# RMSNorm with swish on one core: wider rows for one load and one store, fewer and later stores, and two row sums on ScalarE in every third unit

**Chip, cores, metric.** One core of one Trainium2 chip. The metric is the device time of a run in microseconds, lower is better. "Span" is the profiled time from the first to the last instruction; it lies about 1.3 us under the time of the same run.

## The reference

```python
batch, seq, dim = 16, 1024, 512          # x: fp32, 16384 rows of 512
rms = np.sqrt(np.mean(x ** 2, axis=-1, keepdims=True) + eps)
x_norm = x / rms * gamma
return x_norm * (1.0 / (1.0 + np.exp(-x_norm)))
```

Every row is read once and written once: 33.56 MB in, 33.56 MB out.

## The kernel before

The 16384 rows lie 128 to a "row" of all partitions, so a core-wide row is 2 KB a partition and 256 KB in all; there are 128 of them. They pass through a ring of 96. SyncE issues the loads, ScalarE the stores. The work goes by units of four rows (`cn = 4`, 32 units).

```python
sizes = [4, 4, 8] + [16] * 6 + [8, 8]     # rows of each load, and of the store that answers to it
ring, cn, n_sq = 96, 4, 3
...
def square(k):                            # ScalarE
    t, at, first = chunks[k]
    if first:
        nc.scalar.wait_ge(ld[t], 16)      # the whole load must have landed
    acc = nc.scalar.activation(           # row 3: square and sum in one instruction
        out=junk[k % 2], in_=xb[:, at + n_sq, :], func=AF.Square,
        scale=inv_d**0.5, accum_out=ms[:, k, n_sq : n_sq + 1])
    ...
    square = nc.scalar.activation(        # rows 0 to 2: squares to PSUM
        out=sq[k % 2][:, 0:n_sq, :], in_=xb[:, at : at + n_sq, :],
        func=AF.Square, scale=inv_d**0.5)
...
for k in range(K + 3):                    # ScalarE's order
    if k < K:
        square(k)
    while stored < T and ends[stored] <= k - 2:
        store(stored)                     # waits until its units' Silus are done
        stored += 1
    if 2 <= k < K + 2:
        swish(k - 2)                      # Silu of four rows
...
# VectorE: sums(k), a reduce of the three squared rows, then norm(k - 1), four row multiplies.
# GpSimd: eps and the power -1/2. A load into ring rows in use waits for their stores.
```

## Time and profile before

| | before |
|---|---|
| time | 160.11 us (159.87 to 160.23, 3 runs) |
| span | 158.7 us |
| VectorE, ScalarE busy | 87%, 79% of the span |
| both DMA queues | 99.2% of 16 engines' span, 423 GB/s |

The costliest groups of the page, which the change touches. The columns are line, engine, operation, names and shapes, count, busy us and mean ns, then idle time ahead of them and what ended it.

```profile
L184 ACT ACTIVATE xb<-xb 128x2048 f32<-128x2048 f32 x32 | 61.1, 1909 | 17.8 <-DVE xb L224 17.8
L213 DVE TENSOR_REDUCE ms<-sq 128x3 f32<-128x1536 f32 x32 | 56.1, 1754 | 7.0 <-ACT sq L172 7.0
L165 ACT ACTIVATE junk<-xb 128x512 bf16<-128x512 f32 x32 | 19.7, 615 | 3.4 <-DMA xb<-in_x_dram 3.3
```

VectorE's reduce waits once, at the start. ScalarE has 17.8 us of waits for VectorE ahead of its Silus: some room for more sums. The waits for loads are 3.3 us, all at the start.

### The profile page before, as it was taken

Reading aid. Unit: us, or ns where it says so; the run is one execution under the profiler, and the core shown is the slowest. Engines: PE = TensorE matmul, PEld = TensorE weight load, DVE = VectorE, ACT = ScalarE, POOL = GpSimd, SP = SyncE. Lnnn points to the kernel's source line nnn. Section 1 sums busy time; section 2 is a strip of 40 time slices with the busy share of each in tenths; the row PEclk is TensorE's granted clock in tenths of the full one; section 3 lists DMA queues with packets and bytes.
Section 4 is the critical chain, followed back from the end, with each engine's and each line's share of the span. In section 5 each row is a group of like instructions: output and inputs, shape, how many; then the busy total and the mean of one; then the engine's idle time right before and its main releaser. Section 6 shows DMA issues by size and latency. Waiting matters only on the chain.

```text
span 158.7 us, 439 instructions
## 1 busy us (share of the span) xinstructions
DVE 138.9 (87%) x162; ACT 125.3 (79%) x129; POOL 65.4 (41%) x71
## 2 busy tenths in 40 slices
DVE  0249999999999999999999999999999999999300
ACT  0935989888888889988888888888998888883600
POOL 2035444444455555544444445555544444445000
DMA  7999999999999999999999999999999999999997
GB/s 235 427 523 405 396 450 419 409 452 407 460 394 413 467 421 452 413 396 479 432 413 429 446 429 413 425 417 458 429 454 396 434 446 438 446 413 438 388 458 301
DMA packets 3324, 67.15 MB, mean 423 GB/s; under 512 B 501, under 2 KB 501, under 8 KB 505
## 3 DMA queue, kind: packets, MB, share of 16 engines
q1 hardware_dynamic: 1584, 33.56, 49.9%
q10 hardware_dynamic: 1736, 33.57, 49.3%
q14 instruction: 4, 0.02, 0.0%
HBM read 33.56 MB, written 33.56 MB: 423 GB/s over the span
## 4 chain that ended last, share of the span: by engine, by line
DVE 85%; DMA 5%; ACT 1%; issue 1%; POOL 0%; POOLq 0%
DVE xb L224 53%; DVE ms L213 32%; DMA gamma<-in_gamma_dram 5%; ACT xb L184 1%; DVE gamma_sb L237 0%; POOL gamma L142 0%; POOL blank L141 0%; POOLq L65 0%
## 5 line engine op out<-in xcount | busy, mean ns | idle before, releaser
L224 DVE SCALAR_TENSOR_TENSOR xb<-xb,rstd,gamma_sb 128x512 f32<-128x512 f32 x128 | 87.4, 748 | 0.0
L184 ACT ACTIVATE xb<-xb 128x2048 f32<-128x2048 f32 x32 | 61.1, 1909 | 17.8 <-DVE xb L224 17.8
L213 DVE TENSOR_REDUCE ms<-sq 128x3 f32<-128x1536 f32 x32 | 56.1, 1754 | 7.0 <-ACT sq L172 7.0
L147 POOL TENSOR_SCALAR aeps<-ms 128x4 f32<-128x4 f32 x32 | 20.6, 644 | 75.2 <-DVE ms L213 75.2
L172 ACT ACTIVATE sq<-xb 128x1536 f32<-128x1536 f32 x32 | 45.9, 1433 | 0.0
L154 POOL TENSOR_TENSOR rstd<-aeps,neg_half 128x4 f32<-128x4 f32 x32 | 44.0, 1376 | 2.7
L165 ACT ACTIVATE junk<-xb 128x512 bf16<-128x512 f32 x32 | 19.7, 615 | 3.4 <-DMA xb<-in_x_dram 3.3
L165 ACT ACTIVATION_READ_ACCUMULATOR junk<-xb 128x1 f32 x32 | 6.0, 186 | 0.0
L199 ACT ACT_TABLE_LOAD x1 | 1.3, 1283 | 3.6 <-issue 3.6
L237 DVE LOAD_MASK_SELECT gamma_sb<-gamma x1 | 0.0, 14 | 2.3 <-DMA gamma<-in_gamma_dram 2.3
L141 POOL MEMSET blank<- 128x16 f32 x1 | 0.1, 111 | 1.5 <-POOLq L65 1.5
L237 DVE STREAM_SHUFFLE gamma_sb<-gamma 128x512 f32<-128x512 f32 x1 | 0.7, 717 | 0.0
L142 POOL MEMSET gamma<- 128x512 f32 x1 | 0.5, 524 | 0.0
L264 POOL MEMSET const-float32-0.0<- 128x1 f32 x1 | 0.1, 98 | 0.2 <-issue 0.2
L264 POOL MEMSET const-bfloat16-1.0<- 128x1 bf16 x1 | 0.1, 102 | 0.0
L264 POOL MEMSET const-uint8-127<- 128x1 uint8 x1 | 0.1, 101 | 0.0
L143 POOL MEMSET neg_half<- 128x4 f32 x1 | 0.1, 101 | 0.0
L264 POOL MEMSET const-float32-1.0<- 128x1 f32 x1 | 0.1, 98 | 0.0
## 6 DMA issues: line engine op xcount, KB each, us to landing
xb<-in_x_dram SPq DMA_DIRECT2D x6, 4096.0 KB, 41.9
out_dram<-xb ACTq DMA_DIRECT2D x6, 4096.0 KB, 31.1
xb<-in_x_dram SPq DMA_DIRECT2D x3, 2048.0 KB, 35.0
out_dram<-xb ACTq DMA_DIRECT2D x3, 2048.0 KB, 10.7
xb<-in_x_dram SPq DMA_DIRECT2D x2, 1024.0 KB, 5.8
out_dram<-xb ACTq DMA_DIRECT2D x2, 1024.0 KB, 20.8
scratch<-blank ACTq DMA_DIRECT2D x1, 8.0 KB, 7.7
gamma<-in_gamma_dram ACTq DMA_DIRECT2D x1, 8.0 KB
```

Source lines behind the costliest of these rows:

```text
L141: nc.gpsimd.memset(blank, 0.0).then_inc(s_blank, 1)
L142: nc.gpsimd.memset(gamma4, 0.0).then_inc(s_zero, 1)
L147: nc.gpsimd.tensor_scalar(out=aeps[:, k, :], in0=ms[:, k, :], scalar1=eps_f, scalar2=None, op0=ALU.add,),
L154: nc.gpsimd.tensor_tensor(out=rstd[:, k, :], in0=aeps[:, k, :], in1=neg_half, op=ALU.pow),
L165: acc = nc.scalar.activation(out=junk[k % 2], in_=xb[:, at + n_sq, :], func=AF.Square, scale=inv_d**0.5, accum_out=ms[:, k, n_sq : n_sq + 1],)
L172: square = nc.scalar.activation(out=sq[k % 2][:, 0:n_sq, :], in_=xb[:, at : at + n_sq, :], func=AF.Square, scale=inv_d**0.5,)
L184: nc.scalar.activation(out=rows, in_=rows, func=AF.Silu), s_norm, k + 1
L199: nc.scalar.preload_act_table_set("silu_and_others")
L213: nc.vector.tensor_reduce(out=ms[:, k, 0:n_sq], in_=sq[k % 2][:, 0:n_sq, :], op=ALU.add, axis=mybir.AxisListType.X,),
L224: ins = nc.vector.scalar_tensor_tensor(out=row, in0=row, scalar=rstd[:, k, j : j + 1], in1=gamma_sb, op0=ALU.mult, op1=ALU.mult,)
L237: nc.vector.stream_shuffle(gamma_sb, gamma4, [0] * 32), s_gld, 16
L264: nc = _bacc.Bacc("TRN2", target_bir_lowering=False, num_devices=1)
```

## The change

Its intent: relieve VectorE, which has no gap, by one row in every third unit, and move the same bytes in fewer and larger packets (11 loads and 11 stores become 9 and 8). Loads and stores no longer pair; groups of up to 48 rows lie together in HBM. Below, a "64 KB row" is what one partition moves in a transfer of 32 of the kernel's rows (32 x 2 KB).

```diff
-    sizes = [4, 4, 8] + [16] * 6 + [8, 8]
+    groups = [16, 48, 32, 16, 16]
+    loads = [(0, 0, 4), (0, 4, 4), (0, 8, 8), (1, 0, 16), (1, 16, 16), (1, 32, 16),   # group, row, rows
+        (2, 0, 32), (3, 0, 16), (4, 0, 16)]
+    stores = [(0, 0, 16), (1, 0, 32), (1, 32, 16), (2, 0, 16), (2, 16, 16), (3, 0, 16),
+        (4, 0, 8), (4, 8, 8)]
-    n_sq = 3
+    def n_sq(k):
+        return 2 if k % 3 == 2 else 3
 ...
+        rows = ap[begin[g] * P : (begin[g] + groups[g]) * P]
+        return rows.rearrange("(p n) d -> p n d", n=groups[g])[:, r : r + n, :]
 ...
-        acc = nc.scalar.activation(out=junk[k % 2], in_=xb[:, at + n_sq, :], ...)
+        for j in range(n, cn):
+            acc = nc.scalar.activation(out=junk[j % 2], in_=xb[:, at + j, :], ...)
```

(Cut to its core: the semaphores, the waits for ring rows and the store's arguments follow the lists.)

## The prediction

> **What bounds the kernel now.** I read the page from the top: engines, then the 40 slices, then the chain that ended last, then the DMA queues. The first and the third seem to say VectorE.
>
> ```profile
> span 158.7 us, 439 instructions
> DVE 138.9 (87%) x162; ACT 125.3 (79%) x129; POOL 65.4 (41%) x71
> ...
> DMA  7999999999999999999999999999999999999997
> ...
> DMA packets 3324, 67.15 MB, mean 423 GB/s; under 512 B 501, under 2 KB 501, under 8 KB 505
> ...
> q1 hardware_dynamic: 1584, 33.56, 49.9%
> q10 hardware_dynamic: 1736, 33.57, 49.3%
> ...
> DVE 85%; DMA 5%; ACT 1%; issue 1%; POOL 0%; POOLq 0%
> ```
>
> VectorE has no gap between 11.0 us and 148.15 us: the chain repeats four row multiplies (2.65 us) and one reduce (1.67 us), 4.32 us for a unit of four rows, 32 times. But the two DMA queues add up to 99.2% of 16 engines' span, and the DMA row is full in every slice but the first and last. Two resources are saturated together. Which of them sets the end is read where VectorE stops: the stretches of the trace, with columns for the stretch, its length, busy VectorE, ScalarE and GpSimd, granted clock, DMA share and GB/s, and the last instructions in order of time.
>
> ```profile
> 60.00:130.00 70.00, 70.00 (x82) 62.74 (x65) 32.73 (x33) 1.00 1.01 433
> 130.00:157.00 27.00, 18.14 (x23) 15.58 (x15) 8.16 (x8) 1.00 0.99 427
> ```
> ```profile
> 143.15 0.34 ACTq L189 DMA_DIRECT2D out_dram<-xb  x1
> ...
> 148.17 1.91 ACT L184 ACTIVATE xb<-xb 128x2048 f32<-128x2048 f32 x1 [0.74 <-DVE xb L224]
> 150.11 0.34 ACTq L189 DMA_DIRECT2D out_dram<-xb  x1
> ```
>
> VectorE and ScalarE are done at 150.1, yet the DMA stays full at 427 GB/s to 157. By the semaphores' landings in the trace the last four stores end at 139.3, 149.0, 153.8 and 158.7 us: 9.7 us for the second (16 rows a partition, 4 MB) and 4.85 us for each of the last two (8 rows, 2 MB). The last store was issued at 150.1, three microseconds before the one ahead of it had landed. So stores are queued at the end, and the DMA engines, not VectorE, set the time. The record of single packets agrees: summed over both queues, the packets of one engine take 157.4 us, and the time from the first packet (1.0 us) to the end of the last (158.3) is 157.3 us.
>
> **What a packet costs.** In the same record one packet is one partition's row of a transfer: 8 KB take 309 ns, 16 KB 611 ns, 32 KB 1213 ns (medians; loads and stores alike). The differences give 302 ns per 8 KB, that is 27.2 GB/s for an engine, and some 8 ns for the packet itself. 64 KB should take about 2418 ns (my extrapolation).
>
> **What the Trainium skill says.** (1) "DMA: Bandwidth & Descriptors", section "Where 436 GB/s comes from": 16 ports of 32 B at 850 MHz give 435.2 GB/s. The trace agrees: 433 GB/s from 60 to 130 us, and 27.2 GB/s an engine. Nothing is left to win on the rate. (2) The same page, "Queues, rings and completion order": each engine takes turns between queue rows, one packet at a time. The trace agrees: while 32 KB loads meet 8 KB stores (24 to 44 us) the shares are near four to one, in the next lines (queue, packets, MB, share); with 32 KB on both sides they are near equal (64 to 78 us: 49.3% and 52.2%).
>
> ```profile
> q1 hardware_dynamic: 224, 6.82, 78.9%
> q10 hardware_dynamic: 226, 1.72, 20.3%
> ```
>
> (3) "VectorE: DVE Perf Modes", "Rules for kernel authors": a reduce runs at 1x; with that page's 0.96 GHz, 512 elements are 533 ns. The trace fits: 1754 ns for 1536 elements is 1600 plus 154. (4) "ScalarE: Activation LUTs", "What ACT_TABLE_LOAD costs": 0.833 ns per element, so a row is 427 ns. The trace fits: 1433 ns for 1536 and 1909 for 2048 differ by 476 for 512, the two writing to different memories.
>
> **The change, part by part.**
>
> Row sums: units 2, 5, ... 29, ten in all, reduce two rows instead of three. VectorE loses 10 x 0.533 = 5.3 us. ScalarE gains ten accumulating squares (615 + 186 ns, of which about 0.19 overlaps, so 0.61 us by their distance from the next square) and loses ten rows of the plain square (0.43 us): +0.19 us a unit, +1.9 us of elapsed work, about +3.7 us in its busy sum. Would ScalarE hold VectorE up? Now ScalarE waits 0.46 us a unit before its Silu, and works 3.86 of 4.32 us. Where VectorE's interval shrinks to 3.79 us and ScalarE still owes the next unit 3.86 us plus handover, I expect a stall of about 0.2 us, once in three units: 0 to 2 us. VectorE then ends at 148.15 - 5.3 + (0 to 2) = 142.8 to 144.8 us, if no load is late.
>
> Transfers: per engine, eight packets for each transfer. Before: 32 of 8 KB, 48 of 16 KB, 96 of 32 KB: 32 x 309 + 48 x 611 + 96 x 1213 = 155.66 us. After: loads 16 of 8 KB, 8 of 16 KB, 40 of 32 KB, 8 of 64 KB; stores 16 of 16 KB, 40 of 32 KB, 8 of 64 KB: 16 x 309 + 24 x 611 + 80 x 1213 + 16 x 2418 = 155.33 us. Saving 0.33 us. Five transfers fewer drop five semaphore writes of 9 ns on each engine, 0.05 us. All of this lies on the saturated path. The bytes are the same.
>
> Does the queue stay full? My own reckoning, with 0.605 us per row of all partitions (1213 ns x 8 / 16). The first store now goes out after four units, near 30.5 us instead of 18.0; loads fill the time. It shares with loads until about 52 us and frees the first ring rows. The 32-row load then runs alone; the 32-row store is issued near 63.5 us and takes equal turns with it in 64 KB packets. That load lands near 75 us and unit 16 wants it at 78.3 (its time now) - 5 x 0.53 = 75.6: tight. Meanwhile the store's other rows meet the 16-row load at two to one, to about 95 us; then the last load is released, lands near 120 us, and is wanted at 125. From there four stores and a remainder queue up. The last store is issued at 145 to 147 us, or 149 with a stall at unit 16, while its turn comes only near 153. At no point do I find an empty queue.
>
> Sum: 160.11 - 0.33 - 0.05 = 159.7 us. The 5.3 us of VectorE are hidden behind transfers and become a longer wait of the last store.
>
> **The rivals.**
>
> VectorE is the bound: the chain gives it 85% of the span, and it has no gap. Then 5.3 us less gives 154.8, or 156.8 with the stalls. Against it: 67.1 MB at 435.2 GB/s alone are 154.2 us, plus 1.0 before the first packet, plus the packets' 8 ns and the slow first ones (8 KB loads average 354 ns rather than 309), plus 1.4 us between span and time. The chain is followed to an instruction and does not show the queue behind the last store.
>
> The 32-row load comes late: unit 16 stalls, ScalarE is held in its queue, two Silus and a store behind it wait. For: my reckoning leaves 0.5 us. Against a loss: at that time the 32-row store keeps the DMA busy for some 20 us, and the end has 4 to 8 us of slack. Even 3 us of stall leaves 159.7; only some 8 us would show, giving 161 to 163.
>
> 64 KB packets are worse than extrapolated (split, or slower in HBM because group pieces now lie 96 KB apart). At 3% on the 32 rows each way, 64 of 256 rows, that is 1.2 us: 160.9. Nothing in the profile speaks for it, as 8 to 32 KB are linear; nothing shows 64 KB either.
>
> Smaller transition costs: packets over the median cost about 0.7 us after the first 5 us, most of it between 20 and 50 us where stores first meet loads. Later, larger stores may save or add 0.3 us of that.
>
> **Range and chances.** Point 159.7. Transitions and spread of runs (159.87 to 160.23) give 0.4 either way, the packet rival stretches the top: 159.0 to 160.6. Over 2% faster needs 156.9, under what the bytes and the start allow in practice: 2%. Over 2% slower needs 163.3, thus an idle DMA of 3 us: 3%. Within: 95%.
>
> **What would show it.** Right: DMA full in every middle slice, both queues near 98.5 to 99.5% together, 2604 packets (3324 less 720), 64 KB packets near 2418 ns, VectorE's busy time near 133.6 us and ScalarE's near 129, the last Silu ending near 145 to 147 and the last store taking 11 to 14 us to land instead of 8.6. Wrong: a DMA slice below 9 in the middle, a last store that lands within 7 us of its issue (then compute sets the end), or 64 KB packets above 2450 ns.

## The result

The changed kernel takes 162.63 us (162.19 to 162.86, 4 runs) against 160.17 (159.87 to 160.28): a ratio of 1.0153, 95% interval 1.0127 to 1.018. Executions over 1.5% slower than the fastest of the same kernel are left out of the means. Ratios here are the mean time of one kernel's fast runs over that of the other's of the same rounds, so not quite the ratio of the medians quoted. The change costs 1.5%; the prediction had 159.7 and at most 160.6.

The page of the changed kernel:

```profile
span 161.5 us, 451 instructions
DVE 134.5 (83%) x162; ACT 126.4 (78%) x149; POOL 65.4 (41%) x71
...
DMA  7999999989999979969999999999999999999994
...
DMA packets 2603, 67.15 MB, mean 416 GB/s; under 512 B 420, under 2 KB 420, under 8 KB 424
...
q1 hardware_dynamic: 1296, 33.56, 49.8%
q10 hardware_dynamic: 1304, 33.57, 48.5%
...
DVE 55%; ACT 25%; DMA 5%; issue 4%; another core or an unknown queue 3%; POOL 0%; ACTq 0%; POOLq 0%
```

The two queues have 720 packets fewer, as intended, and VectorE is busy 4.4 us less. The DMA row has an 8, a 7 and a 6 in the middle, which by the letter is one of the prediction's signs of being wrong. But the row books a packet's whole time in the slice where it begins, and a 64 KB packet takes 2.4 us of a slice of 4.0. Counted by overlap from the record of packets, no slice between the first and the last is under 0.98. So the DMA has work up to the last slice and still sets the end, but the rate fell from 423 to 416 GB/s, and its last slice is at 4 where it was at 7. The share of q10 and q1 is now 98.3%. The stretches of the trace where this arises, before:

```profile
66.00:106.00 40.00, 40.00 (x48) 35.92 (x38) 19.56 (x19) 1.00 0.99 428
156.00:158.00 2.00, 0.00 (x0) 0.00 (x0) 0.00 (x0) 1.00 0.79 336
158.00:160.00 2.00, 0.00 (x0) 0.00 (x0) 0.00 (x0) 1.00 0.00 0
```

and after (the share of engines is next to last, GB/s last; a packet is counted where it begins):

```profile
66.00:106.00 40.00, 34.72 (x42) 32.23 (x38) 16.42 (x17) 1.00 0.97 401
106.00:130.00 24.00, 23.70 (x30) 22.48 (x28) 12.26 (x12) 1.00 1.00 433
158.00:160.00 2.00, 0.00 (x0) 0.00 (x0) 0.00 (x0) 1.00 0.67 287
160.00:162.00 2.00, 0.00 (x0) 0.00 (x0) 0.00 (x0) 1.00 0.02 8
```

Two things are to be seen. From 66 to 106 us, while the 64 KB store takes turns with loads, the DMA counts as busy and moves 401 GB/s instead of 428. From 106 us on it is at 433 again. And at the end the engines stop one after another: 0.67 of them busy, then 0.02.

The record of single packets says the same. A packet's excess is its time over the median of its size. Summed and divided by 16 it grew from 1.42 to 3.17 us an engine, of which 1.6 us lie between 85 and 106 us. From 66 to 106 us alone the excess was 0.1 us before and is 1.9 now, and most of that is not on the 64 KB packets: 1.13 us fall on the 32 KB loads (1339 ns in the mean there), 0.46 on the 64 KB stores, 0.32 on the last 64 KB loads. The last store's 16 landings (one from each engine) came from 157.90 to 158.66 us before and from 158.98 to 161.41 after: the first engine finishes 1.1 us later, the last 2.75 us later. I rebuilt which engine ran which packet by joining each packet to the one whose end it follows (the trace does not name the engine, so this is exact only where ends differ). By that, the mean engine ends at 159.60 us instead of 157.94 (+1.66) and the last at 161.08 instead of 158.29 (+2.79, which is the 2.75 us of the span).

VectorE gained nothing, because the 32-row load came late. The waits of the changed kernel (engine and line, waited for, total us, times, longest) and the order of time around unit 16:

```profile
DVE ms L229 <- ACT sq L187: 12.2, 4, 7.0
ACT junk L178 <- DMA xb<-in_x_dram: 8.8, 4, 5.3
```
```profile
77.58 0.63 ACT L178 ACTIVATE junk<-xb 128x512 bf16<-128x512 f32 x1 [5.35 <-DMA xb<-in_x_dram]
...
79.67 1.76 DVE L229 TENSOR_REDUCE ms<-sq 128x3 f32<-128x1536 f32 x1 [4.84 <-ACT sq L187]
```
```profile
150.00 1.91 ACT L199 ACTIVATE xb<-xb 128x2048 f32<-128x2048 f32 x1 [0.74 <-DVE xb L240]
151.94 0.34 ACTq L204 DMA_DIRECT2D out_dram<-xb  x1
```

The load's 16 landings came from 73.3 to 77.5 us, and the unit needs all of them. ScalarE waits 5.35 us for it, VectorE 4.84 us for ScalarE, and the last store is issued at 151.9 us, later than before (150.1). This still is not what set the end here: the store ahead of it landed from 154.1 to 156.6 us, so every engine had work.

### The profile page after: what moved, and what is told of

The parts are those of the page before. It is cut to its first block, busy times and chain, and to the rows that moved or that the text cites. A ratio compares the mean times of both kernels' runs of the same rounds, so it can differ in the third digit from the quotient of the medians.

```text
span 161.5 us, 451 instructions
## 1 busy us (share of the span) xinstructions
DVE 134.5 (83%) x162; ACT 126.4 (78%) x149; POOL 65.4 (41%) x71
## 2 busy tenths in 40 slices
DMA packets 2603, 67.15 MB, mean 416 GB/s; under 512 B 420, under 2 KB 420, under 8 KB 424
## 4 chain that ended last, share of the span: by engine, by line
DVE 55%; ACT 25%; DMA 5%; issue 4%; another core or an unknown queue 3%; POOL 0%; ACTq 0%; POOLq 0%
DVE xb L240 35%; DVE ms L229 20%; ACT xb L199 12%; ACT sq L187 9%; DMA gamma<-in_gamma_dram 5%; ACT junk L178 4%; DVE gamma_sb L253 0%; POOL gamma L151 0%; POOL blank L150 0%; ACTq L175 0%; POOLq L69 0%
## 5 line engine op out<-in xcount | busy, mean ns | idle before, releaser
L229 DVE TENSOR_REDUCE ms<-sq 128x3 f32<-128x1536 f32 (+1 forms) x32 | 50.8, 1586 | 13.3 <-ACT sq L187 12.2
L187 ACT ACTIVATE sq<-xb 128x1536 f32<-128x1536 f32 (+1 forms) x32 | 41.6, 1299 | 0.0
L178 ACT ACTIVATE junk<-xb 128x512 bf16<-128x512 f32 x42 | 25.8, 615 | 8.8 <-DMA xb<-in_x_dram 8.8
L178 ACT ACTIVATION_READ_ACCUMULATOR junk<-xb 128x1 f32 x42 | 7.8, 186 | 0.0
## 6 DMA issues: line engine op xcount, KB each, us to landing
out_dram<-xb ACTq DMA_DIRECT2D x2, 2048.0 KB, 10.5
```

The source lines that it names most:

```text
L178: acc = nc.scalar.activation(out=junk[j % 2], in_=xb[:, at + j, :], func=AF.Square, scale=inv_d**0.5, accum_out=ms[:, k, j : j + 1],)
L187: square = nc.scalar.activation(out=sq[k % 2][:, 0:n, :], in_=xb[:, at : at + n, :], func=AF.Square, scale=inv_d**0.5,)
L229: nc.vector.tensor_reduce(out=ms[:, k, 0 : n_sq(k)], in_=sq[k % 2][:, 0 : n_sq(k), :], op=ALU.add, axis=mybir.AxisListType.X,),
```

## The experiments

All kernels are the changed one with its lists edited, so that the kernel before is one case of it; all gave correct results. Diffs are against the changed kernel unless said. My theory (A), from the two traces, was that 64 KB packets stretch at the turns between the queues and put the engines out of step. Rivals were the later first store (B) and ScalarE's sums (C). An engine is out of step when it is in a load while most others are in a store, or the reverse. Runs 1 to 4, 5 to 8, 9 to 12 and 13 to 17 each shared a chip, with the kernel before timed beside them. Of its 50 timed runs in all, 48 took 159.80 to 160.69 us; two, on the chip of runs 9 to 12, took 161.73 and 167.56, so a stray long run needs no wide row.

**1. No 64 KB row.**

```diff
-    loads  = [... (2, 0, 32), ...]
-    stores = [(0, 0, 16), (1, 0, 32), ...]
+    loads  = [... (2, 0, 16), (2, 16, 16), ...]
+    stores = [(0, 0, 16), (1, 0, 16), (1, 16, 16), ...]
```

> The changed kernel with its 32-row load and its 32-row store each cut into two of 16 rows (32 KB packets), all else kept. Theory A (64 KB packets stretch at the turns between queues and spread the engines apart): back to 160.0 to 160.8 us, packets' excess over their medians near 1.5 to 2.2 us an engine instead of 3.2, last store's 16 landings within 1.2 us instead of 2.4. Rival B (the later first store, which is kept here, costs it): stays at 162 to 162.9 us. Rival C (two sums on ScalarE, kept here): stays at 162 to 162.9 us.

160.53 us (160.29 to 160.77), ratio 1.0020 (1.0003 to 1.0037). Excess 1.64 us an engine, landings 158.02 to 158.99. The loss is nearly all gone, with the sums and the late first store kept: B and C fall as main causes.

**2. Three sums on VectorE, 64 KB rows kept.**

```diff
-        return 2 if k % 3 == 2 else 3
+        return 3
```

> The changed kernel with three sums on VectorE in every unit, as before. Theory A and B: 162.2 to 163.2 us, since the DMA sets the end; VectorE ends later, and if unit 16's wait is kept, the last store may be issued near 156 and begin to show, up to 164. Rival C (ScalarE's extra sums cost it): 160.0 to 160.5 us.

160.22, 162.57, 160.43, 161.53, 161.27 and 162.45 us; ratio 1.0076 (1.0032 to 1.012). Neither theory foresaw such a spread. The profiled execution was the fastest. The interval lies above 1, so the wide rows cost time without the sums too, and just below the changed kernel's (1.0127 to 1.018), so the sums may have a part in the loss; how is not shown. Runs 10 and 11 look at this kernel again.

**3. The two sums alone, transfers as before.**

```diff
-    groups = [16, 48, 32, 16, 16]
+    groups = [4, 4, 8, 16, 16, 16, 16, 16, 16, 8, 8]
+    loads = stores = [(i, 0, groups[i]) for i in range(11)]
```

> The kernel before with only the two sums in every third unit; transfers as before. Theory A and B: 159.7 to 160.4 us, VectorE ends 3 to 5 us earlier and the last store waits that much longer. Rival C: 162 us or more. If VectorE were the bound: 155 to 157 us.

160.37 us, ratio 1.0006 (0.9985 to 1.0026). ScalarE's last Silu, which waits for VectorE's last row, and the last store:

```profile
145.67 1.91 ACT L197 ACTIVATE xb<-xb 128x2048 f32<-128x2048 f32 x1 [0.74 <-DVE xb L238]
147.61 0.34 ACTq L202 DMA_DIRECT2D out_dram<-xb  x1
```

Against 148.17 and 150.11 before: the last store is issued 2.5 us earlier (I had expected 3 to 5 for VectorE) and the time stays. Compute is not the bound, and relieving it gains nothing.

**4. One first store of 16 rows (and rows in groups of 16), nothing else of the change.**

```diff
+    groups = [16] * 8, loads of 4, 4, 8, then 16 each, 8, 8; stores of 16, ..., 16, 8, 8; n_sq = 3
```

> The kernel before with one first store of 16 rows in place of 4, 4 and 8 (groups of 16 rows), three sums in every unit, no 64 KB row. Theory A: 160.0 to 160.7 us. Rival B (loads alone until 30 us, then a 32 KB store meets them: the 0.7 us stretch at 33 us in the changed kernel): 161 to 162.6 us.

160.70 us, ratio 1.0032 (1.001 to 1.0053): 0.3%, and the cost of the first store meeting the loads is seen (0.9 us of excess from 25 to 60 us, against 0.5 from 10 to 60 before). Not all of the 0.3% is that: the last 8-row load came at 136.8 us and the last store ran late. B is a small part.

**5. Same pieces and packets, other distance in HBM.**

```diff
-    groups = [16, 48, 32, 16, 16]
+    groups = [16, 32, 16, 32, 16, 16]      # the 64 KB rows of the store now lie one behind the other
```

> The changed kernel with the same pieces, order and packet sizes, but the group of 48 rows cut into groups of 32 and 16, so that the 64 KB store rows lie one behind the other in HBM (64 KB from partition to partition, not 96 KB). Theory P (the 96 KB pitch makes store packets collide in HBM): falls to 160.0 to 160.8 us and the excess of the 64 KB store packets between 85 and 105 us goes. Theory A (64 KB turns as such): stays at 161.8 to 163 us.

161.93 us (161.24 to 163.27), ratio 1.0121 (1.0088 to 1.0154). Lower than the changed kernel on that chip (run 8), intervals apart, but two thirds of the loss stay. The distance is not the main cause.

**6. Only the 64 KB store.** The load is cut in two as in run 1.

> The changed kernel with only the 32-row load cut in two; the 64 KB store stays. Unit 16 should no longer wait (its 16 rows land near 62 us, the time wanted is 72). If the 64 KB store, or its meeting with 32 KB loads, makes the loss: 161.5 to 163 us. If the late 64 KB load makes it: 160.2 to 160.8 us, like the run without 64 KB rows.

162.09 us (161.5 to 162.77), ratio 1.0124 (1.0101 to 1.0147). The store alone makes most of the loss. In the profiled execution 14 engines ended by 158.3 us, two at 159.6 and 159.8.

**7. Only the 64 KB load.** The store is cut in two as in run 1.

> The changed kernel with only the 32-row store cut in two; the 64 KB load stays, now meeting 32 KB stores from 47 us on, so it takes two thirds of the turns and lands near 68 to 72 us. If the 64 KB load makes the loss: 161.5 to 163 us. If the 64 KB store does: 160.2 to 160.8 us. If both are needed: both this and the run with the store alone stay under 161 us.

161.18 us (161.0 to 162.06), ratio 1.0084 (1.0064 to 1.0105). A loss, but another one. The load, two thirds of the turns or not, landed at 78.9 us, unit 16 waited 6.7 us, and the last store was issued at 153.4. Stretches of this kernel:

```profile
153.00:156.00 3.00, 0.00 (x0) 0.34 (x1) 0.00 (x0) 1.00 0.74 311
156.00:158.00 2.00, 0.00 (x0) 0.00 (x0) 0.00 (x0) 1.00 1.14 483
158.00:160.00 2.00, 0.00 (x0) 0.00 (x0) 0.00 (x0) 1.00 0.41 172
```

The DMA share falls to 0.74 of 3 us; by overlap the mean engine is idle for 0.6 us from 153 to 155, and for another 0.6 near 138, ahead of an earlier store. The last store lands 6.3 us after its issue, all engines within 0.15 us (159.49 to 159.64), and the packets' excess is only 1.58 us. Here compute sets the end, by way of the late load.

**8. The changed kernel again.**

> The changed kernel itself once more, on the same chip as these runs, for a second trace. All theories: 162.2 to 162.9 us, excess of packets near 3 us an engine, unit 16 waiting some 5 us for the 32-row load. If the slow turns are a matter of chance in the engines' phase (as three sums with 64 KB rows, 160.2 to 162.6, suggest), some of its six runs will lie under 161.5.

162.85 to 163.14 us (4 runs), ratio 1.0180 (1.0167 to 1.0194). Excess 2.62 us, landings 158.16 to 161.49. No run under 161.5, so this kernel loses each time, while run 2's loses at times. By the rebuilt order the mean engine ends here at 158.91 us (+0.97 over the kernel before) and the last at 161.17: the same loss as in the first trace, with a larger part of it in the spread.

**9. A second 64 KB store.**

```diff
     loads as in run 1
-    stores = [..., (2, 0, 16), (2, 16, 16), ...]
+    stores = [..., (2, 0, 32), ...]
```

> No 64 KB load, but a second 64 KB store (the two stores of 16 rows after it joined into one of 32 rows, issued near 113 us while the last load runs until about 125). If 64 KB store rows meeting 32 KB loads stretch packets on some engines: at or above the run with one such store (162.1), 162.0 to 163.5 us, with new excess after 113 us. If that run's loss was only the phase in which its one store began: no more than 162.1, and no excess after 113 us.

161.82 us (161.16 to 162.07), ratio 1.0093 (1.0073 to 1.0113). No more than with one such store, and no excess from 106 to 130 us. My dose argument failed: the second store, of whose 128 packets 44 began before the last load packet, costs nothing that can be seen.

**10 and 11. Two more looks at run 2's kernel.**

> The changed kernel with three sums in every unit, a second time, to look at one execution; its six earlier ones spread from 160.2 to 162.6 us and the one profiled was the fastest. If the slowest engine's stretched packets set the time: an execution of 162 us or more shows a last store whose 16 landings spread over 2 us or more and an engine with 3.5 us of excess or more; one under 160.7 shows a spread near 1 us and at most 2.2 us.

> The same kernel a third time, same expectation: time less 159.1 us should be near the excess of the slowest engine less 1.5 us, within 0.6 us.

162.70 and 163.62 us, two long executions to set beside run 2's of 160.22. The program is the same but the chip is not: the first lies by the top of run 2's fast runs (162.57), the second over it. In the first, VectorE never waited for a late load and the last store was issued at 149.9 us. Its end:

```profile
156.00:158.00 2.00, 0.00 (x0) 0.00 (x0) 0.00 (x0) 1.00 0.73 311
158.00:160.00 2.00, 0.00 (x0) 0.00 (x0) 0.00 (x0) 1.00 0.17 74
160.00:162.00 2.00, 0.00 (x0) 0.00 (x0) 0.00 (x0) 1.00 0.04 16
```

A sixth of the engines are at work from 158 to 160 us. Thirteen engines ended at 158.2 us or earlier, down to 157.3, three between 160.1 and 161.0. The mean engine ended at 158.1 us (158.0 in the short one), with 1.8 us of excess (1.7); so the slowest, by its end, had some 4.7 us (2.3). The landings spread over 3.7 us (0.94). This is the plainest view of the loss: one program, the same mean, 2.5 us more for three late engines. In the second, one engine ended at 161.9 and the other 15 at 159.6 to 159.7. There the last store was issued at 153.8, after a late load; by the rebuilt order the 15 were idle for 0.9 to 2.3 us before it and the late one not at all. So both losses of runs 6 and 7 are in it, but the late engine alone set the time.

**12. A try at something better than both.**

```diff
+    groups = [16] * 8; loads and stores of 4, 4, 8, then 16 each, 8, 8; two sums in every third unit
```

> A try at a version better than both: rows in groups of 16, loads of 4, 4 and 8 rows from one group (the changed kernel's start, whose first packets had 0.5 us of excess against 0.7), early stores of 4, 4 and 8 rows as before (which met the loads with 0.5 us in all against 0.7 to 1.1), no 64 KB row, two sums in every third unit. 159.8 to 160.2 us, so at best 0.2% under the kernel before and likely not clear of it.

160.16 us, ratio 0.9999 (0.9987 to 1.0011). Equal to the kernel before. No version beat it.

Open after twelve runs was whether the 64 KB store does harm by its size or by the empty store queue ahead of it (about 56 to 64 us), after which stores begin anew beside loads (theory G).

**13. The gap without 64 KB rows.**

```diff
     loads and stores as in run 1
+    ends[1] = ends[2]        # rows 16 to 31 are stored only when rows 32 to 47 are done too
```

> No 64 KB row at all, but the store of rows 16 to 31 held back until the unit at which the changed kernel's 64 KB store goes out (near 64 us), so the store queue is empty from about 56 to 64 us as it is in the changed kernel. Theory G (stores that begin anew beside a stream of loads put the engines out of step): 161.3 to 162.5 us, landings of the last store over 2 us apart. Theory A' (the gap alone is harmless, 64 KB packets are needed): 160.3 to 160.8 us, landings within 1.3 us.

160.39 us (160.25 to 160.66), ratio 1.0020 (1.0008 to 1.0032); landings 157.85 to 159.30, 1.45 us apart where I had expected 1.3 at most. The gap is nearly harmless.

**14. The 64 KB store without the gap.**

```diff
     loads as in run 1, stores as in the changed kernel
+    ends[0] = 8              # the first store is held back and still runs when the 64 KB store is issued
```

> The run with the 64 KB store and no 64 KB load, but the first store held back to unit 8 (near 47 us), so that it still runs when the 64 KB store is issued at 64 us and the store queue has no gap. Theory G: 160.2 to 160.9 us. Theory A': 161.5 to 162.8 us, as with the gap.

163.62 us (163.27 to 164.13), ratio 1.0222 (1.0204 to 1.0241); excess 3.15 us, landings 159.16 to 161.91. Worse than with the gap, which I had not expected. Theory G falls; of the two it is the wide rows. Why holding back the first store costs more is not shown.

**15. Run 6 again, as control.**

> Control on this chip: the kernel with the 64 KB store, no 64 KB load, gap kept. 161.5 to 162.8 us as before under either theory.

Fast runs 160.64 to 162.31 us, ratio 1.0090 (1.0053 to 1.0127), and one of 163.75 counted as slow. It is as scattered as run 2; I had not expected runs as low as 160.64. Runs 13 and 15 are the closest pair of all: the same chip, the same loads, and 8 MB of stores that go out at the same unit, as two transfers of 32 KB rows or as one of 64 KB rows. So neither the gap nor the amount that is queued makes the loss. The width of a row and the size of a transfer still change together; no run separates them.

**16. Store packets of 48 KB.**

```diff
     loads as in run 1
-    stores = [(0, 0, 16), (1, 0, 32), (1, 32, 16), ...]
+    stores = [(0, 0, 16), (1, 0, 24), (1, 24, 24), ...]
```

> No 64 KB row; the group of 48 rows is stored as 24 and 24 (48 KB packets) while the loads stay at 16 rows or fewer. If the loss grows with the size of the store packet: between, 160.8 to 162 us. If it needs 64 KB: 160.2 to 160.8 us.

Fast runs 163.65 to 165.52 us, ratio 1.0290 (1.0252 to 1.0327), two more runs at 166.99 and 168.37. Neither branch came true: two stores of 48 KB rows cost more than one of 64 KB rows. They meet loads one after the other here, from 56 to 115 us. The profile fell on the slowest run and shows another end than the runs above: the last store is issued at 160.8 us and lands everywhere within 0.15 us, after loads that landed only at 115.1 and 136.9 us, and the DMA stood nearly idle from about 138 to 146. The store of rows 64 to 79 had landed on its first engine at 127.7 us and on its last at 137.1. The fast runs have no trace, so the reason of their loss stays open, and this run says nothing sure about the width of rows.

**17. Only a late 64 KB store.**

```diff
     loads as in run 1
-    stores = [(0, 0, 16), (1, 0, 32), (1, 32, 16), (2, 0, 16), (2, 16, 16), ...]
+    stores = [(0, 0, 16), (1, 0, 16), (1, 16, 16), (1, 32, 16), (2, 0, 32), ...]
```

> Stores of 16 rows as in the run without 64 KB rows, but those of the group of 32 joined into one 64 KB store, issued near 113 us beside the last load only (to about 127 us), then alone. If every 64 KB store that takes turns with 32 KB loads loses in proportion to its turns: a third of its packets do, 160.6 to 161.2 us. If only the early, longer one does: 160.2 to 160.6 us. If the 64 KB store alone is enough: 161.5 us or more.

160.30 us, ratio 1.0014 (0.9999 to 1.0028). It costs nothing measurable. But the trace shows that this run did not test what I meant: the store's first packet began at 118.8 us and the last load packet at 118.7, so no wide row took turns with a load. In the changed kernel all 128 packets of the 64 KB store, from 67.7 to 95.9 us, began while loads were running. A wide store that meets no load is harmless; how much meeting it takes to do harm, run 9's second store (44 of 128 packets, no loss seen) bounds only from one side.

The runs by their last store's landings (us of the profiled execution, so beside that execution's time):

| kernel | time | first, last landing |
|---|---|---|
| before | 160.02 | 157.90, 158.66 |
| changed | 162.77 | 158.98, 161.41 |
| 1, no 64 KB | 160.35 | 158.02, 158.99 |
| 17, late 64 KB store | 160.31 | 157.91, 158.95 |
| 2, three sums, short | 160.22 | 157.92, 158.86 |
| 10, three sums, long | 162.70 | 157.64, 161.34 |
| 6, 64 KB store | 161.50 | 157.96, 160.14 |
| 8, changed, again | 162.85 | 158.16, 161.49 |
| 7, 64 KB load | 161.00 | 159.49, 159.64 |

Where the first landing stays near 158 and the last moves, some engines are late; where both move together (run 7), the last store came too late. In the first trace of the changed kernel both the first moves (all engines are later) and the spread grows.

**What goes with the stretching.** For each 64 KB store packet I counted how much of the other engines' time beside it went to stores too. In runs 6, 8 and 10, packets beside 80% or more of stores had a mean excess of 5, 2.5 and 1 ns (119, 50 and 102 packets), the others 130, 107 and 208 ns (9, 78 and 26 packets); in the changed kernel's first trace 15 packets had 0 and 113 had 65 ns. In run 1, with 32 KB packets, the store packets have none at any share. So the wide store packets that stretch belong to an engine out of step with the others. Not every such packet stretches: in run 2's profile 21 of them had 0.4 ns, and in run 5's 14 had 3 ns, though its landings still spread over 2.0 us. The 32 KB loads, which carry more of the excess, were not sorted this way. This is an association from the rebuilt order, not a mechanism: what in the chip slows packets, and why a given execution falls out of step, stays open.

## Why the prediction was wrong

**What bounds it: right.** The DMA sets the end, VectorE does not. Run 3 shows it: 2.5 us taken from compute, no change in time. The first rival (VectorE as the bound, 154.8 to 156.8) is out.

**The step that failed** is the sum, "160.11 - 0.33 - 0.05", with the working under "Transfers" that it rests on. It summed packets of one engine at their medians, took the excess as fixed, and let all 16 engines end together. The medians held to the nanosecond (64 KB: 2418 ns). The means did not: 64 KB loads 2459 ns, 64 KB stores 2475, and all 32 KB loads 1260 instead of 1225 (1339 from 66 to 106 us). So the excess, for which the prediction allowed a change of 0.3 us either way, grew by 1.75, and the mean engine ended 1.66 us later in place of the forecast fall. And the end is the slowest engine's, which the sum had no term for: another 1.13 us of spread (2.79 - 1.66). In run 8, the same kernel, the two parts were 0.97 and 1.90 us. Run 10 shows the second term alone, as its mean engine is no later than in run 2's short execution.

**The rival that was nearest** was "64 KB packets are worse than extrapolated". I gave it 1.2 us and a chance that hardly widened the range, and named the wrong ways (split, or the 96 KB distance). The 64 KB store without the 64 KB load costs 0.9 to 1.2% (runs 6 and 15); the distance is a third of the changed kernel's loss at most (1.2% in run 5 against 1.8% in run 8). "Nothing in the profile speaks for it" was true and a poor reason: the profile before holds no 64 KB packet, and packets of up to 32 KB were all that its straight line covers.

**The late load: the mechanism right, the hour wrong.** I put the want at 75.6 us and the landing at 75, and took a wait for possible. ScalarE was ready at 72.2 us and the load landed at 77.5. I had named the units one too far: in the kernel before, unit 16 begins near 74.0 us and not 78.3 (the store issued at 48.2 us goes out with unit 10, and six units of 4.32 us follow). So the wait was 5.35 us, the last store was issued at 151.9 instead of the forecast 145 to 149, and landed 9.5 us later, not 11 to 14. I was right that this slack covers it in the changed kernel, but only just: in run 7 it did not, and the DMA fell idle.

**The sums.** The reduce of two rows costs what was worked out:

```profile
L229 DVE TENSOR_REDUCE ms<-sq 128x3 f32<-128x1536 f32 x22 | 38.6, 1754 | 13.3 <-ACT sq L187 12.2
L229 DVE TENSOR_REDUCE ms<-sq 128x2 f32<-128x1024 f32 x10 | 12.2, 1217 | 0.0
```

537 ns a unit against 533. The stall behind ScalarE, forecast at 0 to 2 us, takes more: three units last 12.65 us instead of 12.95 in the chain, so 0.3 of the 0.54 us remain, and run 3 ended VectorE 2.5 us earlier instead of 3.3 to 5.3. ScalarE's busy time is 126.4 us and not 129, because the page counts overlapping instructions once: their durations added up grew by 3.6 us (133.9 to 137.4), close to the 3.7 of the forecast. The 476 ns that the prediction took as a fit for 427 compared two memories; the squares into PSUM, of 1536 and now also of 1024 elements, take 1433 and 1005 ns, which is 428 for a row. In run 3 none of this reaches the time.

**What was checked and held:** packets (2603 of 2604 forecast), a DMA that is full in the middle by overlap, medians of packets. **What should have warned:** my own criterion "DMA full in every middle slice" misleads both ways. The page's row fails it (8, 7, 6) only by where it books long packets, and a DMA that is busy and slow meets it; GB/s over the stretch (401) is the better one. Of the other two signs, the last store took 9.5 us and not under 7, and 64 KB packets were over 2450 ns in their mean, not in their median.

## What to carry to other kernels

Where the DMA queues are full from end to end, as here, work taken from a compute engine buys nothing (run 3), and the time is that of the slowest of the 16 DMA engines: compare the first and the last of a transfer's 16 landings before trusting a sum of packet times. Wider rows saved 8 ns a packet here and cost 1.4 us or more where such a store took turns with loads for some 28 us; stores in 32 KB rows were safe, and a wide row where the loads were over or nearly so (runs 17 and 9). A large load also lands as a whole, so the first unit that needs any of it waits for the last byte, and that eats the slack that other parts of a change have made.

## What the Trainium skill lacked or had wrong

- "DMA: Bandwidth & Descriptors", "Rules for kernel authors", and "SBUF — State Buffer", "The DMA setup-cost knee", advise large transfers, the latter the largest single transfer possible. Here one store of 8 MB in 64 KB rows beside loads cost 0.9 to 1.2% over the kernel before, and the same 8 MB as two stores in 32 KB rows 0.2% (runs 6, 15 and 13). No page has an upper limit for rows where loads and stores take turns.
- No page says how far apart the DMA engines of one transfer can end where loads and stores take turns, or that packets stretch there: the last store's landings spread by 0.8 us before and by 2.4 and 3.3 us in the two traces of the changed kernel, for the same bytes on each engine.
- "DMA: Bandwidth & Descriptors", "Queues, rings and completion order", speaks of turns after a packet of some 9 to 17 descriptors. In these traces an engine changes queue after one partition's row, of 8 to 64 KB: two 32 KB streams alternate row by row, and 32 KB rows against 8 KB rows give shares of 78.9% and 20.3%. How many descriptors a row is, the traces do not show.
- The same page's "Measured" section has about 10.5 ns a packet as a floor, from a transfer of 4 KB issued another way, and nothing for wide rows; here a packet costs some 8 ns beyond its bytes, for loads and stores alike (309, 611, 1213 and 2418 ns for 8 to 64 KB).
